# Two FFN down projections: eight of eleven double inner blocks as products of a seven-product block scheme

## The chip, the cores and the metric

The kernel runs on one core of one Trainium2 chip. The time is the device time of one launch in microseconds (us); the median of several runs is compared. Engines are named as in the profile: PE (TensorE), PEld (its weight loads), DVE (VectorE), ACT (ScalarE), POOL (GpSimd), SP (SyncE, which issues most DMAs).

## The reference

One encoder layer over two requests with the same weights, 256 and 512 tokens, D = 1024, D_FF = 2816, all in float32:

```python
x = layer_norm(a * x + 0.5 * swiglu(x, ffn1_w_gu, ffn1_w_down))
x = layer_norm(a * x + parallel_mixer(x, ...))
x = layer_norm(a * x + memory_cross_attention(x, mem, ...))
x = layer_norm(a * x + 0.5 * swiglu(x, ffn2_w_gu, ffn2_w_down))

def swiglu(x, w_gu, w_down):
    gate, up = jnp.split(x @ w_gu, 2, axis=-1)
    return (jax.nn.silu(gate) * up) @ w_down
```

The parts that matter here are the two down projections: h (768 x 2816) times w_down (2816 x 1024).

## The kernel before

All 768 tokens (512 of stream S and 256 of stream P) are worked on together. A float32 product is made of three matmuls in the format fp32r: each operand is split into a high part (cast by ACT, L87, tiles wh, hq, Vh) and a low part (operand minus high part, L88, by DVE or POOL, tiles wl, hq), and high x high, high x low and low x high are added in PSUM.

An FFN (`ffn_fast`, n = 1 or 2) has 22 inner blocks j of 128 hidden columns. For each j, a gate/up block (`block`, `products`) computes gate and up by a seven-product scheme: seven products of 12 matmuls 128x384, in the order P1, P5, P6, P3, P7, P2, P4. ACT copies partial sums out of PSUM (tiles snap), DVE adds (sum), ACT takes silu (sil), DVE multiplies (h), and `gated` splits h into hq (high by ACT, low by POOL) and sends it to DRAM (hspill, 768 KB), all but the last four j, which stay in SBUF (`keep`). Weights of the next block come in two loads of 512 KB (raw); `weights_of` makes sums of their halves on DVE (tiles tt, L330 to L338) and splits seven operands of 128x512, five low parts on DVE and two (P3, P2) on POOL. The first blocks (j = 0 to 2) of the first FFN are plain blocks beside the preparation of the token sums (tiles S1 to S4, L1096 to L1102); that part is called its front.

The down projection follows directly. A double inner block kp is two j's. Its weights are two halves of 512 output columns, each a load of 512 KB (raw, `load_w`) split by ACT (wh) and POOL (wl). `down_group` takes groups of blocks ([9, 10, 0], [1, 2, 3], [4, 5]): for each half it adds all blocks of the group in six PSUM banks (one per tile of 128 tokens; dn), 36 matmuls 128x512 per block and half, then DVE adds the banks to acc (L211, L213). Blocks other than 9 and 10 first read their hidden tiles back (hr, 768 KB). `down_last` does the last three blocks [6, 7, 8] tile by tile, with the layer norm of a finished tile beside the matmuls of the next. acc's old values (the residual) come in six loads issued by ACT.

The order on each engine is set by the tile framework that builds the program: it places instructions by dependencies and its own estimate of when they can start. SP works its queue in that order, and an instruction that waits holds up those behind it. Pools are given back tile by tile (`reuse_waits="tile"`), so a load into a new pool can wait for the last reader of the tile that had the memory before.

The mixer, between, starts with the same kind of seven-product blocks (tiles mS1 to mS4, acc as scratch) and `values()`, which makes V from weights split by ACT and POOL and is copied out of PSUM by DVE.

Of the kernel before, what the change touches and what calls it, by code (L numbers as in the profile page):

```python
# [7 lines left out]
F32 = mybir.dt.float32  # L8
# [50 lines left out]
def _encoder(ctx, tc, nc, io, out, dbg):  # L59
# [161 lines left out]
    def down_group(wdn, kps, hh, hl, first, after_loads=None):  # L221

        for half in range(2):
            pss = {(s.name, t): psum(nid("dn")) for s in STREAMS for t in range(s.nt)}
            for kp in kps:
                w = load_w(wdn[kp, half])
                for s in STREAMS:
                    for t in range(s.nt):
                        down(pss[s.name, t][:], s, t, w, kp, hh, hl, kp == kps[0], kp == kps[-1])
            if half == 0 and after_loads:  # L230
                after_loads()
            for s in STREAMS:
                for t in range(s.nt):
                    add_acc(s, t, half, pss[s.name, t][:], first)

    def down_last(wdn, kps, hh, hl, fp, i):

# [52 lines left out]
    def seven(X, pool, more, tt, snap_t, sum_t):  # L290

        unit = [None, None, 2]
        turn = [0]

        def raw():
            turn[0] += 1
            if (turn[0] - 1) % (3 + more) < 3:
                return wp.tile([128, 1024], F32, tag="raw", bufs=3, name=nid("raw"))
            return pool.tile([128, 1024], F32, tag="raw", bufs=more, name=nid("raw"))


# [12 lines left out]
        lo, hi = slice(0, 512), slice(512, 1024)  # L314

        def weights(wg, wu):

            rg, ru = raw(), raw()
            for r, w in ((rg, wg), (ru, wu)):
                if len(w.shape) == 4:  # L320
                    r4 = r[:].rearrange("p (a b c) -> p a b c", a=4, b=2)
                    for z in range(2):
                        nc.sync.dma_start(r4[:, :, z, :], w[:, :, z, :])
                else:
                    nc.sync.dma_start(r[:], w)
            V, G = nc.vector, nc.gpsimd
            t = [tt() for _ in range(4)]
            b = {}
            b["P1"] = operand(rg[:, lo], V)
            V.tensor_tensor(t[0], rg[:, lo], ru[:, lo], op=ALU.add)  # L330
            b["P5"] = operand(t[0], V)
            V.tensor_tensor(t[1], t[0], ru[:, hi], op=ALU.add)
            b["P6"] = operand(t[1], V)
            b["P3"] = operand(ru[:, hi], G)
            V.tensor_tensor(t[2], ru[:, lo], ru[:, hi], op=ALU.add)  # L335
            b["P7"] = operand(t[2], V)
            b["P2"] = operand(rg[:, hi], G)
            V.tensor_tensor(t[3], t[1], rg[:, hi], op=ALU.add)  # L338
            b["P4"] = operand(t[3], V)
            return b  # L340

        LEFT = {"P1": "A11", "P2": "A12", "P3": "S4", "P4": "A22", "P5": "S1", "P6": "S2", "P7": "S3"}

        def product(p, b, ps, start):
            tiles(X[LEFT[p]], b[p], ps, start)

        def tiles(a, w, ps, start, ks=range(4)):
            (ah, al), (wh, wl) = a, w
            for k in ks:
                c = slice(k * 128, (k + 1) * 128)  # L350
                st, sp_ = start and k == 0, k == 3
                for n, (l, r) in enumerate(((wh, ah), (wh, al), (wl, ah))):
                    nc.tensor.matmul(ps, l[:, c], r[:, k, :], start=st and n == 0, stop=sp_ and n == 2,  # L353
                                     skip_group_check=True)

        def snap(ps, nm):
            t = snap_t()
            ins = nc.scalar.activation(t, ps, AF.Copy)
            if nm == "p1":
                marks["act"] = ins.ins  # L360
            return t

        def added(ps, t, nm):
            o = sum_t()
            ins = nc.vector.tensor_tensor(o, t, ps, op=ALU.add)  # L365
# [24 lines left out]
        return operand, weights, tiles, products, (lo, hi)  # L390

    def ffn_fast(n, i, front, order6, src, groups, last):

        wgu, wdn = io[f"ffn{n}_gu"], io[f"ffn{n}_dn"]
        dr = dp.tile([128, NFB, 2, TT], F32, name=f"hspill{n}")
        right = ExitStack()
        hp = right.enter_context(tc.tile_pool(name=f"hkeep{n}", bufs=1, reuse_waits="tile", side="right"))
        left = ExitStack()
# [28 lines left out]
            marks["dve"] = ins.ins  # L427
            gated(j, h32)

        def gated(j, h32, eng=nc.gpsimd):  # L430
            q = hp.tile([128, 2, TT], F32R, tag="hq", bufs=4, name=nid("hq"))
            split(q[:, 0, :], q[:, 1, :], h32[:], eng)
            keep[j] = q
            if j < NFB - 4:
                nc.sync.dma_start(dr[:, j, :, :], q[:].bitcast(F32))

        def plain_weights(j):
            rg, ru = [wp.tile([128, 1024], F32, tag="raw", bufs=3, name=nid("raw")) for _ in range(2)]
# [23 lines left out]
            gated(j, h32)  # L462

        nx, ws = front(locals())
        for j in range(nx, NFB):
            block(j, ws)
            if j + 1 < NFB:
# [12 lines left out]
        def place(j, q):  # L480
            for s in STREAMS:
                for t in range(s.nt):
                    c = order6.index(s.t0 + t) * 128
                    hh[s.name, t, j], hl[s.name, t, j] = q[:, 0, c:c + 128], q[:, 1, c:c + 128]

        with tc.tile_pool(name=f"down{n}", bufs=1, reuse_waits="tile") as f2:
            for j in range(NFB - 4, NFB):
                place(j, keep[j])

            def load_h(js):  # L490
                for j in js:
                    q = f2.tile([128, 2, TT], F32R, tag="hr", bufs=6, name=nid("hr"))
                    nc.sync.dma_start(q[:].bitcast(F32), dr[:, j, :, :])
                    place(j, q)

            def load_acc():
                for t in range(6):
                    late_load(acc_[:, t, :], src[:, t, :])

            for gi, kps in enumerate(groups):  # L500
                load_h([j for kp in kps for j in (2 * kp, 2 * kp + 1) if j < NFB - 4])
                down_group(wdn, kps, hh, hl, gi == 0, None if gi else load_acc)
            load_h([j for kp in last for j in (2 * kp, 2 * kp + 1)])
            down_last(wdn, last, hh, hl, f2, i)
        right.close()


    def mixer(i):
# [53 lines left out]
        for b in (0, 2, 1, 3):  # L562
            small(b, H2, ws[b])

        def values(ts):
# [12 lines left out]

        slots = [o_[:, t, :] for t in range(6)] + [v_[:, t, :] for t in range(3, 6)]
# [37 lines left out]
        values(range(3))  # L617
# [496 lines left out]
    def front2(env):  # L1114
# [22 lines left out]
        quarters(X)  # L1137
        w2 = load_w(wgu[2]) + load_w(wgu[NFB + 2])
        for k in range(4):
            x0 = hp.tile([128, 2, TT], F32, tag="hq", bufs=4, name=nid("x0"))  # L1140
# [5 lines left out]
            sums(X, (env["snap_t"], env["sum_t"]), k, *a)  # L1146
        w3 = env["weights"](3)
        for j in range(2):
            env["gated"](j, h01[j], nc.vector)
        env["plain_block"](2, w2)  # L1150
        return 3, w3

    ffn_fast(1, 0, front1, [0, 2, 4, 1, 3, 5], io["x_tok"], ([9, 10, 0], [1, 2, 3], [4, 5]), [6, 7, 8])
    mixer(1)
    x3 = dp.tile([128, 6, D], F32, name="x3")
    with tc.tile_pool(name="lnx", bufs=1) as lp, tc.tile_pool(name="xa", bufs=1, reuse_waits="tile") as ap:
# [128 lines left out]
```

## Time and profile before

| | |
|---|---|
| median of 3 runs | 1823.75 us (1823.02 to 1828.21) |
| the profiled run | 1826.76 us, its span 1824.9 us, granted clock 0.994 |
| PE / PEld busy | 1796.2 us (98%) / 1647.8 us (90%) |
| DVE / ACT / POOL busy | 1154.2 (63%) / 716.1 (39%) / 640.6 us (35%) |
| DMA moved | 236.85 MB, mean 130 GB/s |
| POOL L88 wl<-raw,wh, all forms | 228 operations, 478.8 us |
| PE dn matmuls, the group of L106, L107, L108 | 438 each, 169 us each |

The profiled run is compared with its own span plus 1.9 us around it. Busy shares are averages over stages: PE is near 100% in nearly all of 40 slices, and what a slice waits for is read from the chain of waits and from the timeline. Times in a row of the timeline are the start in us from the span's start and the length in us; in brackets stands the idle time before and what ended it. Lengths of matmuls overlap, so their pitch is taken from start to start.

### The profile page before, as it was taken

How to read it: one execution, taken by the hardware profiler on the slowest of the kernel's cores; microseconds unless marked ns; L12 is line 12 of the kernel's file. 1: busy time of each engine (PE TensorE's matmuls, PEld its weight loads, DVE VectorE, ACT ScalarE, POOL GpSimd, SP SyncE). 2: the span in 40 equal slices, each digit the busy share in tenths (PEclk: the TensorE clock that was granted, in tenths of full speed). 3: DMA queues.
4: the chain of work that ended last, by engine and by line, in shares of the span. 5: the costliest groups of instructions: out<-in, count | busy, mean ns of one | idle time of the engine just before them, and what ended most of it. 6: DMA issues, size and time to landing. Idle time of an engine off the chain costs nothing.

```text
span 1824.9 us, 25380 instructions
## 1 busy us (share of the span) xinstructions
PE 1796.2 (98%) x9902; PEld 1647.8 (90%) x9902; DVE 1154.2 (63%) x1743; ACT 716.1 (39%) x1235; POOL 640.6 (35%) x362
## 2 busy tenths in 40 slices
PE   9999999999999999999999999999999999999998
PEld 8999999888889999888888888889899999998886
DVE  8788888212479554578654943485697788861136
ACT  6445444211135444555222254335354444441111
POOL 3333333432225112522244253243553333342212
PEclk9999999999999999999999999999999999999999
DMA  5333332635332333311363252246333333336441
GB/s 190 134 122 122 131 130 86 254 127 173 129 117 65 127 133 123 125 36 47 116 231 116 68 198 70 81 172 186 121 116 134 122 122 122 122 105 251 162 140 69
DMA packets 69335, 236.85 MB, mean 130 GB/s; under 512 B 7744, under 2 KB 13120, under 8 KB 69216
## 3 DMA queue, kind: packets, MB, share of 16 engines
q1 hardware_dynamic: 64032, 220.04, 35.1%
q10 hardware_dynamic: 5184, 15.21, 2.2%
q8 instruction: 77, 1.26, 0.3%
q14 instruction: 42, 0.34, 0.1%
HBM read 189.60 MB, written 45.61 MB: 129 GB/s over the span
## 4 chain that ended last, share of the span: by engine, by line
PE 71%; DVE 9%; ACT 1%; issue 1%; DMA 0%; POOL 0%; DVEq 0%; ACTq 0%
PE px L353 13%; PE py L353 7%; PE dn L108 7%; PE dn L107 7%; PE dn L106 7%; PE pt L107 4%; PE pt L106 4%; PE pt L108 4%; PE pz L353 3%; PE to L108 2%; PE to L107 2%; PE to L106 2%; DVE acc L172 1%; PE pp L353 1%; PE V L106 1%; PE V L107 1%
## 5 line engine op out<-in xcount | busy, mean ns | idle before, releaser
L88 POOL TENSOR_TENSOR wl<-raw,wh 128x1024 fp32r<-128x1024 f32 (+1 forms) x228 | 478.8, 2102 | 805.3 <-ACT wh L87 748.8
L87 ACT ACTIVATE wh<-raw 128x512 fp32r<-128x512 f32 (+2 forms) x313 | 260.5, 833 | 509.0 <-PE dn L108 195.2
L88 POOL TENSOR_TENSOR hq<-h,hq 128x768 fp32r<-128x768 f32 x42 | 86.1, 2050 | 252.5 <-ACT hq L87 132.6
L106 PE MATMUL pt<-xh,wh 128*128 128x512 f32 (+2 forms) x512 | 173.4, 339 | 0.0
L107 PE MATMUL pt<-xl,wh 128*128 128x512 f32 (+2 forms) x512 | 172.6, 337 | 0.0
L108 PE MATMUL pt<-xh,wl 128*128 128x512 f32 (+2 forms) x512 | 172.2, 336 | 0.0
L106 PE MATMUL dn<-wh,hr 128*128 128x512 f32 (+1 forms) x438 | 169.4, 387 | 0.0
L107 PE MATMUL dn<-wl,hr 128*128 128x512 f32 (+1 forms) x438 | 169.2, 386 | 0.0
L108 PE MATMUL dn<-wh,hr 128*128 128x512 f32 (+1 forms) x438 | 169.1, 386 | 0.0
L88 DVE TENSOR_TENSOR wl<-raw,wh 128x512 fp32r<-128x512 f32 (+2 forms) x85 | 111.8, 1320 | 82.9 <-ACT wh L87 82.8
L88 DVE TENSOR_TENSOR wl<-tt,wh 128x512 fp32r<-128x512 f32 x156 | 132.0, 882 | 4.5 <-ACT wh L87 3.9
L213 DVE TENSOR_TENSOR acc<-acc,dn 128x512 f32<-128x512 f32 (+1 forms) x73 | 49.2, 678 | 126.8 <-PE dn L108 126.6
L87 ACT ACTIVATE wh<-tt 128x512 fp32r<-128x512 f32 x156 | 93.5, 624 | 71.9 <-POOL wl L88 48.2
L106 PEld LDWEIGHTS pt<-xh,wh 128*128 128x128 f32 x512 | 97.4, 190 | 9.8 <-issue 0.5
L108 PEld LDWEIGHTS pt<-xh,wl 128*128 128x128 f32 x512 | 97.2, 190 | 9.0
L107 PEld LDWEIGHTS pt<-xl,wh 128*128 128x128 f32 x512 | 97.3, 190 | 8.7 <-issue 0.2
L107 PEld LDWEIGHTS dn<-wl,hr 128*128 128x128 f32 x438 | 82.3, 188 | 16.7
L106 PEld LDWEIGHTS dn<-wh,hr 128*128 128x128 f32 x438 | 82.3, 188 | 16.7
L108 PEld LDWEIGHTS dn<-wh,hr 128*128 128x128 f32 x438 | 82.3, 188 | 16.5
L425 DVE SCALAR_TENSOR_TENSOR h<-sil,sum 128x384 f32<-128x384 f32 x78 | 53.1, 683 | 61.3 <-ACT sil L424 61.3
L335 DVE TENSOR_TENSOR tt<-raw 128x512 f32<-128x512 f32 x39 | 87.8, 2252 | 0.0
L353 PE MATMUL px<-xh,wh 128*128 128x384 f32 x232 | 78.3, 337 | 2.5 <-DVE sum L365 2.5
(360 smaller groups left out, 4747.7 us busy)
## 6 DMA issues: line engine op xcount, KB each, us to landing
raw<-in_ffn_gu_dram SPq DMA_DIRECT2D x84, 512.0 KB, 3.5
hspill<-hq SPq DMA_DIRECT2D x36, 768.0 KB, 3.2
hr<-hspill SPq DMA_DIRECT2D x36, 768.0 KB, 5.5
raw<-in_ffn_dn_dram SPq DMA_DIRECT2D x44, 512.0 KB, 3.5
raw<-in_w_mix_dram SPq DMA_DIRECT2D x32, 512.0 KB, 3.5
raw<-in_w_xk_dram SPq DMA_DIRECT2D x16, 512.0 KB, 3.5
raw<-in_w_xv_dram SPq DMA_DIRECT2D x16, 512.0 KB, 4.0
raw<-in_w_xq_dram SPq DMA_DIRECT2D x16, 512.0 KB, 3.6
```

The lines of the kernel that those rows point to most:

```text
L87: nc.scalar.activation(hi, src, AF.Copy)
L88: (lo_eng or nc.vector).tensor_tensor(lo, src, hi.bitcast(F32), op=ALU.subtract)
L106: nc.tensor.matmul(o, lh, rh, start=start, stop=False)
L107: nc.tensor.matmul(o, lh, rl, start=False, stop=False)
L108: nc.tensor.matmul(o, ll, rh, start=False, stop=stop)
L172: nc.vector.scalar_tensor_tensor(Ah, Ah, mv[:, 0:1], g[h][:], ALU.subtract, ALU.mult)
L213: nc.vector.tensor_tensor(A, A, ps, op=ALU.add)
L335: V.tensor_tensor(t[2], ru[:, lo], ru[:, hi], op=ALU.add)
L353: nc.tensor.matmul(ps, l[:, c], r[:, k, :], start=st and n == 0, stop=sp_ and n == 2, skip_group_check=True)
L425: ins = nc.vector.scalar_tensor_tensor(h32[:, half * HT:(half + 1) * HT], sil[:], -0.5, u, ALU.mult, ALU.mult)
```

## The change

Three things change.

1. **`down_seven`** takes the place of `down_group`. Blocks 9, 10 and 1 to 6 are done as four pairs of the list groups ((9,10), (1,2), (3,4), (5,6); the loop writes one pair per index d). Each kp's two j's, two token halves of 384 (three tiles; order6 lists them) and two column halves form 2x2 blocks, and seven products take the place of eight: 18 matmuls 128x512 per product and pair. `direct` operands are hidden tiles (kept for d = 0, else read back, ao, 768 KB), `summed` operands are sums of hidden blocks (read back as sr, 384 KB, and split by ACT and DVE into ao). A weight quadrant is one load of 512 KB (128x2x512, in pieces of 2 KB); sums of quadrants are made on DVE in T (or in the loaded tile), and all low parts are made on DVE. Three sets of PSUM banks (x, z, y) take the products; `add` puts them into acc. `down_last` does [0, 7, 8]; its hidden tiles are loaded by `ahead()` before the last product.
2. **`gated`** makes the sums after every odd j of a paired block: four DVE operations 128x384 (hs) and four spills of 192 KB (sspill). hq's low part is made on DVE. The spills of the last pair are collected in `late` and are written, in the code, behind the first two products.
3. **POOL's seven-product work goes to DVE**: the low parts of P3 and P2 in gate/up blocks and mixer blocks, and of the first `values()`; `values()` is copied out of PSUM by ACT. acc comes in four lots of three loads of 256 KB.

Of the diff, with what is unchanged left out:

```diff
+    def down_seven(n, wdn, pairs, keep, dr, sd, order6, load_acc, late, ahead):
...
+            raw = [pool.tile([128, 1024], F32, name=nid("raw7")) for _ in range(2)]
+            T = {d: pool.tile([128, 1024], F32, name=nid("T")) for d in range(nd)}
+            bank = [psum(nid("dn")) for _ in range(8)]
+            x, z, y = bank[0:3], bank[3:6], bank[6:8] + bank[3:4]
...
+            def loaded(q, d):
+                turn[0] += 1
+                if turn[0] % 5 < 2:
+                    r = raw[turn[0] % 5]
+                else:
+                    r = wp.tile([128, 1024], F32, tag="raw", bufs=3, name=nid("raw"))
...
+            def direct(t, par, d):
+                if d == 0:
+                    return [keep[2 * kp + par][:, t] for kp in pairs[d]]
+                a = ring()      # ao, 4 buffers
+                nc.sync.dma_start(a[:].bitcast(F32), dr[:, t, par, kp:kp + 2])
...
+            def summed(s, d):
+                r = pool.tile([128, 2, HT], F32, tag="sr", bufs=3, name=nid("sr"))
+                nc.sync.dma_start(r[:], sd[:, s, kp:kp + 2])
+                a = ring()
+                split(a[:, :, 0, :], a[:, :, 1, :], r[:])
...
+            for d in own[:-1]:
+                P1(d)
+                if d == 0:
+                    load_acc(0, 0)
+                P2(d)
+            P2(own[-1])
+            P1(own[-1])
+            for spill in late:
+                spill()
+            for d in early:
+                quadrant(T[d][:], B11, d)
+            load_acc(1, 1)
+            add(0, 0, z)
+            add(0, 0, x)
+            for d in sums_:
+                V.tensor_tensor(T[d][:], T[d][:], loaded(B12, d), op=ALU.add)
+                product(y, summed(0, d), weight(T[d][:]), d == sums_[0], d == sums_[-1])
+            load_acc(0, 1)
+            add(1, 1, y)
+            for d in sums_:
+                b22 = loaded(B22, d)
+                V.tensor_tensor(T[d][:], T[d][:], b22, op=ALU.add)
+                product(x, summed(1, d), weight(T[d][:]), False, d == sums_[-1])
+                if d == sums_[-1]:
+                    add(0, 1, x)
+                product(y, summed(2, d), weight(b22), False, d == sums_[-1])
+            load_acc(1, 0)
+            add(0, 1, y)
+            for d in sums_:
+                b12, b22 = loaded(B12, d), loaded(B22, d)
+                V.tensor_tensor(b12, b12, b22, op=ALU.add)
+                product(x, summed(3, d), weight(b12), False, d == sums_[-1])
+            add(1, 1, x)
+            ahead()
+            for d in own:
+                V.tensor_tensor(T[d][:], T[d][:], loaded(B21, d), op=ALU.add)
+                product(x, direct(1, 1, d), weight(T[d][:]), False, d == own[-1])
+            add(1, 0, x)
...
-            b["P3"] = operand(ru[:, hi], G)
+            b["P3"] = operand(ru[:, hi], V)
-            b["P2"] = operand(rg[:, hi], G)
+            b["P2"] = operand(rg[:, hi], V)
...
+            if par and kp not in last:
+                s_ = [glob["hs"].tile([128, HT], F32, tag="hs", bufs=3, name=nid("hs")) for _ in range(4)]
+                V.tensor_tensor(s_[3][:], a11, a21, op=ALU.subtract)
+                V.tensor_tensor(s_[0][:], a22, a21, op=ALU.subtract)
+                V.scalar_tensor_tensor(s_[1][:], s_[0][:], -1.0, a11, ALU.mult, ALU.subtract)
+                V.scalar_tensor_tensor(s_[2][:], s_[1][:], -1.0, a12, ALU.mult, ALU.subtract)
+                def spill():
+                    for x in (3, 0, 1, 2):
+                        nc.sync.dma_start(sd[:, x, kp, :], s_[x][:])
+                if j == NFB - 1:
+                    late.append(spill)
+                else:
+                    spill()
...
-                w = load_w(io["w_v"][kp])
+                w = load_w(io["w_v"][kp], lo_eng)
-                nc.vector.tensor_copy(v_[:, t, :], ps[:])
+                nc.scalar.activation(v_[:, t, :], ps[:], AF.Copy)
-    ffn_fast(1, 0, front1, ..., ([9, 10, 0], [1, 2, 3], [4, 5]), [6, 7, 8])
+    ffn_fast(1, 0, front1, ..., ((9, 10), (1, 2), (3, 4), (5, 6)), [0, 7, 8])
```

What this makes of the queues shows in the built programs. A name's last number counts tiles; hq, hs and raw are as above.

SP's queue before, from the last loads of gate/up weights of the first FFN into the down projection:

```order
L435 DMA hspill_83<-hq_2775 128x1536
L325 DMA raw_3207<-in_ffn_gu_dram 128x1024
L325 DMA raw_3206<-in_ffn_gu_dram 128x1024
L96 DMA raw_3371<-in_ffn_dn_dram 128x1024
L96 DMA raw_3413<-in_ffn_dn_dram 128x1024
L96 DMA raw_3455<-in_ffn_dn_dram 128x1024
L96 DMA raw_3515<-in_ffn_dn_dram 128x1024
```

SP's queue after, at the same place:

```order
L582 DMA sspill_84<-hs_3140 128x384
L582 DMA sspill_84<-hs_3141 128x384
L238 DMA raw_3550<-in_ffn_dn_dram 128x2x512
L582 DMA sspill_84<-hs_3438 128x384
L582 DMA sspill_84<-hs_3435 128x384
L582 DMA sspill_84<-hs_3436 128x384
L582 DMA sspill_84<-hs_3437 128x384
L238 DMA raw_3459<-in_ffn_dn_dram 128x2x512
L265 DMA ao_3524<-hspill_83 128x1536
```

Before, weights of the down projection follow the last gate/up weights. After, the weights of the second to fourth steps (raw_3498, raw_3522, raw_3550) stand earlier, and the weight of the first step, raw_3459, stands behind the four spills of the last pair. In the second FFN two loads of hr, in two pieces each, stand among these spills as well, the second of them directly ahead of the first step's weight.

DVE before, from the end of the last gate/up block of the first FFN:

```order
L365 TENSOR_TENSOR sum_3323<-snap_3251,pz_3310 128x384
L425 SCALAR_TENSOR_TENSOR h_3337<-sil_3338,sum_3294 128x384
L425 SCALAR_TENSOR_TENSOR h_3337<-sil_3341,sum_3308 128x384
L211 SCALAR_TENSOR_TENSOR acc<-acc,dn_3365 128x512
L211 SCALAR_TENSOR_TENSOR acc<-acc,dn_3366 128x512
```

DVE after, at the same place:

```order
L484 TENSOR_TENSOR sum_3411<-snap_3339,pz_3398 128x384
L545 SCALAR_TENSOR_TENSOR h_3425<-sil_3426,sum_3382 128x384
L545 SCALAR_TENSOR_TENSOR h_3425<-sil_3429,sum_3396 128x384
L576 TENSOR_TENSOR hs_3435<-h_3425,h_3284 128x384
L577 SCALAR_TENSOR_TENSOR hs_3436<-hs_3435,h_3284 128x384
L88 TENSOR_TENSOR hq_3432<-h_3425,hq_3432 128x2x384
L578 SCALAR_TENSOR_TENSOR hs_3437<-hs_3436,h_3425 128x384
L88 TENSOR_TENSOR wl_3474<-raw_3459,wh_3473 128x1024
L88 TENSOR_TENSOR wl_3501<-raw_3498,wh_3500 128x1024
```

The three sums of the last pair and hq's low part now stand between the last h and the low part of the first step's weight (wl_3474), and that ahead of those of the next steps.

DVE before, at the front of the first FFN:

```order
L1100 SCALAR_TENSOR_TENSOR sum_365<-snap_364,x_115 128x384
L1102 TENSOR_TENSOR sum_366<-x_115 128x384
L330 TENSOR_TENSOR tt_495<-raw_491,raw_492 128x512
L88 TENSOR_TENSOR S3l_104<-sum_366,S3h_103 128x384
L332 TENSOR_TENSOR tt_496<-tt_495,raw_492 128x512
L88 TENSOR_TENSOR wl_500<-tt_495,wh_499 128x512
```

DVE after, at the same place:

```order
L1263 SCALAR_TENSOR_TENSOR sum_366<-snap_365,x_116 128x384
L88 TENSOR_TENSOR hq_294<-h_287,hq_294 128x2x384
L1265 TENSOR_TENSOR sum_367<-x_116 128x384
L449 TENSOR_TENSOR tt_496<-raw_492,raw_493 128x512
L88 TENSOR_TENSOR wl_509<-raw_493,wh_508 128x512
L88 TENSOR_TENSOR S3l_105<-sum_367,S3h_104 128x384
L88 TENSOR_TENSOR wl_501<-tt_496,wh_500 128x512
```

hq's low part and the low part of a plain weight half (wl_509), which POOL had, stand in DVE's row.

More of the change, by code (lines that the diff above doesn't have):

```diff
@@ L219, in down, with quadrant, weight, ring @@
             tok_mm(ps, w, kk, hh[s.name, t, j], hl[s.name, t, j], first and kk == 0, stop and kk == 1, cols)
[L221 to L234, printed above, removed]
+    def down_seven(n, wdn, pairs, keep, dr, sd, order6, load_acc, late, ahead):
+        with tc.tile_pool(name=f"seven{n}", bufs=1, reuse_waits="tile") as pool:
+            V = nc.vector
+            nd = len(pairs)
+            raw = [pool.tile([128, 1024], F32, name=nid("raw7")) for _ in range(2)]
+            turn = [0]
+            T = {d: pool.tile([128, 1024], F32, name=nid("T")) for d in range(nd)}
+            bank = [psum(nid("dn")) for _ in range(8)]
+            x, z, y = bank[0:3], bank[3:6], bank[6:8] + bank[3:4]
+            def quadrant(dst, q, d):
+                row, half = q
+                kp = pairs[d][0]
+                nc.sync.dma_start(dst.rearrange("p (a c) -> p a c", a=2),
+                                  wdn[kp:kp + 2, half, :, row * 512:row * 512 + 512].rearrange("a p c -> p a c"))
+            def loaded(q, d):
[4 more added lines that the diff above has]
+                    r = wp.tile([128, 1024], F32, tag="raw", bufs=3, name=nid("raw"))
+                quadrant(r[:], q, d)
+                return r[:]
+            def weight(src):
+                h = wp.tile([128, 1024], F32R, tag="wh", bufs=5, name=nid("wh"))
+                l = wp.tile([128, 1024], F32R, tag="wl", bufs=5, name=nid("wl"))
+                split(h[:], l[:], src)
+                return h, l
+            def ring():
+                return pool.tile([128, 2, 2, HT], F32R, tag="ao", bufs=4, name=nid("ao"))
+            def direct(t, par, d):
+                if d == 0:
+                    return [keep[2 * kp + par][:, t] for kp in pairs[d]]
+                a = ring()
+                kp = pairs[d][0]
+                nc.sync.dma_start(a[:].bitcast(F32), dr[:, t, par, kp:kp + 2])
+                return [a[:, k] for k in range(2)]
+            def summed(s, d):
+                r = pool.tile([128, 2, HT], F32, tag="sr", bufs=3, name=nid("sr"))
+                kp = pairs[d][0]
+                nc.sync.dma_start(r[:], sd[:, s, kp:kp + 2])
+                a = ring()
+                split(a[:, :, 0, :], a[:, :, 1, :], r[:])
+                return [a[:, k] for k in range(2)]
+            def product(ps, a, w, start, stop):
+                wh, wl = w
+                for t in range(3):
+                    c = slice(t * 128, t * 128 + 128)
+                    for k in range(2):
+                        o = slice(k * 512, k * 512 + 512)
+                        ah, al = a[k][:, 0, c], a[k][:, 1, c]
+                        for m, (l, r) in enumerate(((ah, wh), (ah, wl), (al, wh))):
+                            nc.tensor.matmul(ps[t][:], l, r[:, o], start=start and k == 0 and m == 0,
+                                             stop=stop and k == 1 and m == 2, skip_group_check=True)
+            seen = set()
+            def add(c, half, ps):
+                op = ALU.subtract if c == half == 1 or c < half else ALU.add
+                for t in range(3):
+                    A = acc_[:, order6[3 * c + t], half * 512:half * 512 + 512]
+                    if (c, half) in seen:
+                        V.tensor_tensor(A, A, ps[t][:], op=op)
+                    else:
+                        V.scalar_tensor_tensor(A, A, ALPHA, ps[t][:], ALU.mult, op)
+                seen.add((c, half))
+            acc_ = glob["acc"]
+            B11, B21, B12, B22 = (0, 0), (1, 0), (0, 1), (1, 1)
+            own = list(range(nd))
+            sums_ = own[1:] + own[:1]
+            early = own[:2]
+            def P1(d):
+                if d in early:
+                    src = loaded(B11, d)
+                else:
+                    quadrant(T[d][:], B11, d)
+                    src = T[d][:]
+                product(x, direct(0, 0, d), weight(src), d == own[0], d == own[-1])
+            def P2(d):
+                product(z, direct(0, 1, d), weight(loaded(B21, d)), d == own[0], d == own[-1])
+            for d in own[:-1]:
[8 more added lines that the diff above has]
+            for d in early:
+                quadrant(T[d][:], B11, d)
+            load_acc(1, 1)
[25 more added lines that the diff above has]
+            add(1, 0, x)
@@ L464, in ffn_fast @@
         nx, ws = front(locals())
+        glob["hs"] = left.enter_context(tc.tile_pool(name=f"hsum{n}", bufs=1, reuse_waits="tile"))
         for j in range(nx, NFB):
@@ L482, in place, with load_acc, load_h @@
                 for t in range(s.nt):
-                    c = order6.index(s.t0 + t) * 128
-                    hh[s.name, t, j], hl[s.name, t, j] = q[:, 0, c:c + 128], q[:, 1, c:c + 128]
-        with tc.tile_pool(name=f"down{n}", bufs=1, reuse_waits="tile") as f2:
[L487 to L503, printed above, removed]
+                    c = order6.index(s.t0 + t)
+                    x = slice(c % 3 * 128, c % 3 * 128 + 128)
+                    hh[s.name, t, j], hl[s.name, t, j] = q[:, c // 3, 0, x], q[:, c // 3, 1, x]
+        def load_acc(c, half):
+            for t in order6[3 * c:3 * c + 3]:
+                x = slice(half * 512, half * 512 + 512)
+                late_load(acc_[:, t, x], src[:, t, x])
+        js = [j for kp in last for j in (2 * kp, 2 * kp + 1)]
+        hlp = ExitStack()
+        def load_h(js, pool, tag, bufs):
+            for j in js:
+                q = pool.tile([128, 2, 2, HT], F32R, tag=tag, bufs=bufs, name=nid("hr"))
+                for t in range(2):
+                    nc.sync.dma_start(q[:, t].bitcast(F32), dr[:, t, j % 2, j // 2])
+                place(j, q)
+        if n == 1:
+            ahead = lambda: load_h(js[:4], hp, "hq", 4)
+        else:
+            lp = hlp.enter_context(tc.tile_pool(name="hlast", bufs=1, reuse_waits="tile"))
+            ahead = lambda: load_h(js, lp, "hr", 6)
+        down_seven(n, wdn, groups, keep, dr, sd, order6, load_acc, late, ahead)
+        with tc.tile_pool(name=f"down{n}", bufs=1, reuse_waits="tile") as f2:
+            if n == 1:
+                load_h(js[4:], f2, "hr", 2)
             down_last(wdn, last, hh, hl, f2, i)
+        hlp.close()
         right.close()
```

40 lines of the change are left out of this document (28 added, 12 removed).

## The prediction

> **What bounds the kernel now.** I read the page first, then TensorE's waits, then the timeline around the places that the change opens.
>
> ```profile
> PE 1796.2 (98%) x9902; PEld 1647.8 (90%) x9902; DVE 1154.2 (63%) x1743; ACT 716.1 (39%) x1235; POOL 640.6 (35%) x362
> ```
>
> ```profile
> PE px L353 <- ACT snap L358: 6.1, 3, 4.5
> PE K L108 <- DVE wl L88: 3.9, 2, 2.1
> PE px L353 <- DVE sum L365: 2.5, 1, 2.5
> ```
>
> TensorE works in 98% of the span and hardly ever waits (columns: us in total, times, longest). So a removed matmul is worth its pitch, and a new wait of TensorE costs its full length. A matmul's duration overlaps the next one's; the pitch is the distance of the starts:
>
> ```profile
> 360.20 0.39 PE L106 MATMUL dn<-wh,hr 128*128 128x512 f32 x1
> 360.42 0.39 PE L107 MATMUL dn<-wl,hr 128*128 128x512 f32 x1
> 360.65 0.39 PE L108 MATMUL dn<-wh,hr 128*128 128x512 f32 x1
> ```
>
> Two pitches are 0.45 us; a 128x512 matmul costs 0.227 us (0.225 to 0.23).
>
> **Fewer matmuls.** One double inner block takes 2 halves x 2 inner parts x 6 token tiles x 3 = 72 matmuls, a pair 144. Seven products of 3 tiles x 2 x 3 = 18 make 126. Eight pairs in the kernel save 8 x 18 = 144 matmuls: -32.7 us. Matmuls that read kept hidden tiles run a little slower (0.23, starts 339.22 and 339.45 below); their number hardly changes between the versions, so I take nothing, with +7 as the end if all 1008 new ones ran so.
>
> **A new wait at the start of each down projection.** Before, the projection follows the last gate/up block without a gap, because its first weights are asked for 7.6 us earlier:
>
> ```profile
> 331.63 11.55 SPq L96 DMA_DIRECT2D raw<-in_ffn_dn_dram  x4
> ```
>
> ```profile
> 339.04 0.34 PE L353 MATMUL px<-A22h,wl 128*128 128x384 f32 x1
> 339.22 0.39 PE L106 MATMUL dn<-wh,hq 128*128 128x512 f32 x1
> 339.45 0.39 PE L107 MATMUL dn<-wl,hq 128*128 128x512 f32 x1
> ```
>
> In the change the weight of the first product, raw_3459, stands on SP behind the four spills of the last pair's sums, and those wait for DVE work that follows the end of the last block. ACT and DVE have this weight ahead of those of the next products, and TensorE runs in order, so nothing else can start. How long after a block's end (call it E) its last h is done shows at an ordinary block, which ends at 221.84:
>
> ```profile
> 221.67 0.33 PE L353 MATMUL px<-A22h,wl 128*128 128x384 f32 x1
> 221.84 0.33 PE L353 MATMUL px<-A11h,wh 128*128 128x384 f32 x1
> ```
>
> ```profile
> 222.10 0.49 ACT L424 ACTIVATE sil<-px 128x384 f32<-128x384 f32 x1 [0.97 <-PE px L353]
> ```
>
> ```profile
> 222.63 0.56 DVE L425 SCALAR_TENSOR_TENSOR h<-sil,sum 128x384 f32<-128x384 f32 x1 [0.90 <-ACT sil L424]
> 223.10 0.68 DVE L330 TENSOR_TENSOR tt<-raw,raw 128x512 f32<-128x512 f32 x1
> 223.82 0.69 DVE L332 TENSOR_TENSOR tt<-tt,raw 128x512 f32<-128x512 f32 x1
> ```
>
> The steps behind it are priced by these groups (after the bar: busy us and mean ns; the next two by tile: min/median/max ns; the last: KB and us from issue to landing):
>
> ```profile
> L365 DVE TENSOR_TENSOR sum<-snap,pz 128x384 f32<-128x384 f32 x39 | 21.6, 554 | 42.1 <-PE pz L353 42.1
> L88 DVE TENSOR_TENSOR wl<-raw,wh 128x1024 fp32r<-128x1024 f32 x26 | 34.2, 1318 | 59.9 <-ACT wh L87 59.8
> L87 ACT ACTIVATE wh<-raw 128x1024 fp32r<-128x1024 f32 x154 | 163.2, 1060 | 472.6 <-PE dn L108 195.2 <-PE to L108 81.1 <-issue 49.7
> L213 DVE TENSOR_TENSOR acc<-acc,dn 128x512 f32<-128x512 f32 x71 | 48.3, 686 | 124.8 <-PE dn L108 124.7
> ```
>
> ```profile
> L435 SPq DMA_DIRECT2D hspill<-hq x36: 319/327/425, 38.2 to 1580.6; - x36
> L88 DVE TENSOR_TENSOR hq<-h,hq x2: 943/944/944, 1354.5 to 1355.4; 128x768 fp32r<-128x768 f32 x2
> ```
>
> ```profile
> hr<-hspill SPq DMA_DIRECT2D x36, 768.0 KB, 5.5
> raw<-in_ffn_dn_dram SPq DMA_DIRECT2D x44, 512.0 KB, 3.5
> ```
>
> DVE is free for the next operation at E+1.26. Two sums of 0.55 end at E+2.4, hq's low part (0.94) at E+3.3, the last sum at E+3.9. SP issues its spill (0.33) and raw_3459 at E+4.2, which lands 3.5 later at E+7.7. ACT's cast (1.06) brings E+8.8, DVE's low part (1.3) E+10.1. The third matmul needs it and would have started at E+0.47: 9.6 us, some 10.0 with handovers. Behind such a gap the granted clock is halved. Columns as above; first and last of the slow run, and the two behind it, at two gaps of before:
>
> ```profile
> 48.71 0.69 PE L353 MATMUL px<-S2h,wh 128*128 128x384 f32 x1 [4.49 <-ACT snap L358]
> 49.19 0.52 PE L353 MATMUL px<-S2l,wh 128*128 128x384 f32 x1
> ...
> 53.99 0.39 PE L353 MATMUL py<-S4l,wh 128*128 128x384 f32 x1
> 54.22 0.34 PE L353 MATMUL py<-S4h,wl 128*128 128x384 f32 x1
> ```
>
> ```profile
> 597.06 0.69 PE L353 MATMUL px<-xh,wh 128*128 128x384 f32 x1 [2.52 <-DVE sum L365]
> 597.55 0.52 PE L353 MATMUL px<-xl,wh 128*128 128x384 f32 x1
> ...
> 600.11 0.40 PE L353 MATMUL px<-xh,wh 128*128 128x384 f32 x1
> 600.34 0.34 PE L353 MATMUL px<-xl,wh 128*128 128x384 f32 x1
> ```
>
> 16 matmuls at about 0.32 where 0.17 is normal lost 2.4 us; at the second gap 9 lost 1.4. I take 2.1 behind the longer gap: 12.1 us in the first FFN. In the second, two pieces of hr (384 KB each) also stand between the spills and the weight: +0.7 (two issues) to +2 (5.5 against 3.5 above), I take 1.4: 13.5. Together **+25.6**, with ends 17 (each landing 2 us quicker and almost no slow clock) and 31 (landing as hr's, 5.5).
>
> The Trainium skill, "TensorE: Matmul & The Clock Gate", Part 1 on the clock gate, has the clock return after one window of about 3.4 us of work; by that each gap would lose 1.7 us instead of 2.1, and the sum would be 0.8 lower. The rows differ from it on both sides (5.3 and 3.1 us).
>
> **Inside the seven products.** A projection has 28 steps of 18 matmuls, 4.09 us each, 114 us. Beside them DVE has 28 low parts of weights and 16 sums of weights at about 1.3, 16 low parts of summed activations at 0.94 and 21 additions to acc at 0.69: 87 us. DMA moves 30 weights of 0.52 MB, 9 ao of 0.79, 16 sr of 0.39, 12 acc pieces of 0.26 and 6 hr of 0.79: 37 MB. What the queues deliver shows in the start of the first projection before (last column GB/s), where TensorE worked all the time:
>
> ```profile
> 340.00:350.00 10.00, 10.00 (x45) 8.02 (x44) 2.48 (x1) 2.64 (x4) 5.21 (x3) 1.00 0.88 320
> 350.00:360.00 10.00, 10.00 (x45) 8.11 (x44) 1.38 (x2) 1.06 (x1) 3.83 (x2) 1.00 1.01 417
> 360.00:370.00 10.00, 10.00 (x45) 8.16 (x44) 2.75 (x4) 1.06 (x1) 2.41 (x1) 1.00 0.97 375
> ```
>
> At their mean, 371, 37 MB take 100 us of the 114: hidden. The tightest loop is the fourth (sums of both right quadrants): DVE 4 x (1.3 + 0.94 + 1.3) + 6 additions = 18.3 us against 16.4, with buffers filled ahead by the looser loop before. I take **+3** for both projections (ends 0 and +15).
>
> **GpSimd freed.** Where GpSimd and DVE work together, DVE's operations stretch, at both fronts where TensorE waits for DVE:
>
> ```profile
> 36.36 2.20 DVE L1100 SCALAR_TENSOR_TENSOR sum<-snap,x 128x384 f32<-128x384 f32 x1
> ...
> 591.41 4.07 DVE L88 TENSOR_TENSOR wl<-acc,wh 128x512 fp32r<-128x512 f32 x3
> ```
>
> Operations of the first size take 0.55 above, three of the second about 2.1 (0.68 each). At the first FFN's front the change drops the GpSimd work but gives DVE hq's low part and two or three weights' (about 2): of the 4.5 us wait I take 1.5 off, with its slow clock kept (ends +1 and -6.9, all gone). At the mixer's front the wait of 2.5 us and the 1.4 of slow clock go: -4 (ends 0 and -4.5). Together **-5.5**.
>
> **Gate/up blocks.** Two of them, an even and an odd one:
>
> ```profile
> 221.84:250.96 29.12, 29.12 (x169) 29.12 (x169) 23.69 (x28) 13.98 (x26) 10.60 (x6) 1.00 0.37 127
> ```
>
> DVE has 28 operations: undisturbed 18 x 0.72 + 10 x 0.47 = 17.7 us (pitches from 223.10 to 223.82 and 222.63 to 223.10), so 6 are stretch by GpSimd. The change takes the stretch away and adds four low parts of weights (2.9), two of hq (1.9) and four sums (1.9): 24.4 of 29.1. TensorE stays the bound: +0.6 for now and then a late sum in the odd block (ends 0 and +11).
>
> **Sum:** -32.7 + 25.6 + 3 - 5.5 + 0.6 = -9.0 us. The profiled run took 1826.8 us (1824.9 span and 1.9 around it), 3 above the median; I put the difference on the median, 1823.75: **1815 us**.
>
> **Rivals.**
> - *The start waits are shorter.* For it: both landing and clock could be at their low ends, 17 us, and both fronts' waits could go fully. -32.7 + 17 + 3 - 9 = -22: 1802. Against it: the chain of DVE, SP, DMA, ACT, DVE is serial and each link is a row. If the wait does not arise at all, about 1786.
> - *DMA holds the products* (slower than before). 37 MB in 114 us need 323 GB/s; the 320 of the row 340 to 350 is just under it, and a load waits until its buffer is free. At 290 GB/s 37 MB take 128 us, +14 per projection in place of the +3 for both: -9 - 3 + 28 = +16, 1840. It cancels the gain at 308 GB/s (120 us, +6 per projection). Against it: the mean of 371.
> - *DVE holds the odd gate/up blocks*, 0.7 us in each of 16: +11, and the sum is about +2: 1825, no change. Against it: 24.4 of 29.1.
>
> **Chances.** Forecast 0.5 (own range 1807 to 1823), shorter start waits 0.2, DMA 0.15, odd blocks 0.12, others 0.03. A difference below 0.3% (5.5 us) is about what cannot be told from none. Faster by more: 0.2 and 0.7 of the forecast's 0.5, with little else: 0.56. Within: the rest of the forecast and most of the odd blocks, 0.25. Slower: 0.19. The range reaches from 1797, inside the shorter waits, to 1836, inside the DMA rival.
>
> **What would show it.** Matmul count down by 144. TensorE's waits lead with dn on ACT's wh and DVE's wl, twice, 9 to 14 us from the last px to the third dn, half clock behind. SP's issue of that raw some 4 us after the last px. Then steps of 4.1 us without gaps, the front's 2.5 us wait of px on sum gone, DVE's 128x512 group at L335 near 680 ns. I am wrong if the first dn follows px at once (1790), or if dn waits for sr, ao or wl throughout the products.

## The result, and the profile after

The changed kernel takes 1811.0 us (median of 4 runs, 1809.75 to 1814.35), the kernel before 1825.0 us on the same chip: a ratio of 0.992 with a 95% interval of 0.9906 to 0.9935. So it is faster, by 0.8%. The prediction said 1815, and the time lies in its range. The profiled run took 1809.75 us (its span 1808.0 us), 17.0 less than the profiled run before, which took 1826.76. The page's line of engines, and the first rows of TensorE's waits:

```profile
PE 1762.3 (97%) x9758; PEld 1618.6 (90%) x9758; DVE 1216.4 (67%) x2035; ACT 763.8 (42%) x1297; POOL 321.7 (18%) x186
```

```profile
PE dn L284 <- ACT wh L87: 20.8, 2, 11.9
PE px L472 <- ACT snap L477: 4.3, 2, 3.5
PE K L108 <- DVE wl L88: 4.0, 2, 2.3
```

There are 144 matmuls fewer, GpSimd's work is halved, the mixer's wait of px on sum has gone from the list, and two new waits of dn lead it. The timeline around the first of them, where the last gate/up block of the first FFN ends at 336.08 (E, the start of its last matmul and one pitch of 0.17):

```profile
335.90 0.34 PE L472 MATMUL px<-A22h,wl 128*128 128x384 f32 x1
...
336.33 0.49 ACT L544 ACTIVATE sil<-px 128x384 f32<-128x384 f32 x1 [0.97 <-PE px L472]
...
336.86 0.56 DVE L545 SCALAR_TENSOR_TENSOR h<-sil,sum 128x384 f32<-128x384 f32 x1 [0.90 <-ACT sil L544]
...
338.04 2.25 SPq L582 DMA_DIRECT2D sspill<-hs  x3
...
339.39 0.55 DVE L578 SCALAR_TENSOR_TENSOR hs<-hs,h 128x384 f32<-128x384 f32 x1
...
340.39 0.38 SPq L238 DMA_DIRECT2D raw<-in_ffn_dn_dram  x1
...
344.00 1.06 ACT L87 ACTIVATE wh<-raw 128x1024 fp32r<-128x1024 f32 x1 [5.70 <-DMA raw<-in_ffn_dn_dram]
...
345.08 1.23 DVE L88 TENSOR_TENSOR wl<-raw,wh 128x1024 fp32r<-128x1024 f32 x1 [5.15 <-ACT wh L87]
...
345.11 1.22 PE L284 MATMUL dn<-wh,hq 128*128 128x512 f32 x2 [8.87 <-ACT wh L87]
...
346.37 0.79 PE L284 MATMUL dn<-wl,hq 128*128 128x512 f32 x1
```

This is the predicted chain, link by link: last sum done at E+3.9, raw issued at E+4.3, landed at E+7.9, low part ready and the third matmul started at E+10.3 (predicted 10.1). In the second FFN, E is 1621.23, and SP has loads of hr among the spills:

```profile
1625.48 0.94 SPq L653 DMA_DIRECT2D hr<-hspill  x2
1626.76 0.38 SPq L238 DMA_DIRECT2D raw<-in_ffn_dn_dram  x1
...
1632.20 1.06 ACT L87 ACTIVATE wh<-raw 128x1024 fp32r<-128x1024 f32 x1 [8.76 <-DMA raw<-in_ffn_dn_dram]
...
1634.57 0.80 PE L284 MATMUL dn<-wl,hq 128*128 128x512 f32 x1
```

Raw is issued at E+5.5, 1.2 later than in the first FFN, and lands after 5.4 us instead of 3.6: the third matmul starts at E+13.3, 3.0 later.

Once started, the products run without gaps. Busy time by engine in the stretch of the 504 matmuls of the first projection's products, from their first start, in the changed kernel (then granted clock, DMA share, GB/s):

```profile
345.11:462.72 117.61, 117.57 (x504) 96.43 (x505) 79.59 (x82) 44.66 (x47) 4.79 (x2) 0.97 0.84 305
```

504 matmuls at 0.227 are 114.4 us; the 117.6 hold 3.1 of the start (0.8 until the third matmul, 2.3 of slow clock) and next to nothing else. The same view of the two gate/up blocks that answer to those of before, and of DVE's groups (after the bar: total us, mean ns) one of before and two of after:

```profile
222.10:251.22 29.12, 29.12 (x170) 29.12 (x169) 21.99 (x37) 14.20 (x27) 0.00 (x0) 1.00 0.41 147
```

```profile
L335 DVE TENSOR_TENSOR tt<-raw 128x512 f32<-128x512 f32 x39 | 87.8, 2252 | 0.0
```

```profile
L88 DVE TENSOR_TENSOR wl<-tt,wh 128x512 fp32r<-128x512 f32 x156 | 105.5, 689 | 2.2 <-ACT wh L87 0.5
...
L454 DVE TENSOR_TENSOR tt<-raw 128x512 f32<-128x512 f32 x39 | 26.8, 688 | 0.0
```

In the gate/up blocks DVE is busy 22.0 of 29.1 us, 1.7 less than before, with more work: its operations are no longer stretched (L335, now L454, 2252 to 688 ns). That GpSimd's work beside them had stretched them shows in the kernels between, described below: the same group takes 2257 ns in the mean with only hq's low part left on GpSimd (e3), 938 with only P3 and P2 there (e2) and 683 with neither (e9).

Where the time went, by stage. Each stage runs from the first start of its first group of matmuls to that of the next stage's (the last one to the start of the last matmul, some 8 us before the span's end), and the wait at a projection's start from the end of the last px, counted as E above, to the first dn, both from the timelines (us). "Others" is what the change does not touch, from the first FFN's layer norm to the mixer and through the attention. The runs of the experiments below stand beside it.

| stage | before | after | e1 | e2 | e3 | e4 | e5 | e6 | e7 | e8 | e9 |
|---|---|---|---|---|---|---|---|---|---|---|---|
| FFN1 front and blocks | 333.5 | 330.3 | 329.6 | 331.4 | 333.2 | 331.5 | 334.7 | 330.6 | 333.3 | 329.9 | 332.6 |
| wait | 0 | 9.0 | 0 | 9.7 | 0 | 0 | 0 | 9.2 | 0 | 0 | 0 |
| down 1 | 184.2 | 171.4 | 173.2 | 171.5 | 184.2 | 170.0 | 184.2 | 171.4 | 184.3 | 171.9 | 184.2 |
| mixer | 184.0 | 178.9 | 178.9 | 178.3 | 178.9 | 178.9 | 178.3 | 178.9 | 184.0 | 178.9 | 178.9 |
| FFN2 front | 56.0 | 54.0 | 54.0 | 54.0 | 56.0 | 54.0 | 56.0 | 54.0 | 56.0 | 54.0 | 56.0 |
| FFN2 blocks | 275.9 | 276.8 | 276.8 | 277.8 | 275.8 | 276.8 | 275.9 | 276.8 | 276.2 | 276.8 | 275.9 |
| wait | 0 | 12.1 | 0 | 11.4 | 0 | 0 | 0 | 9.4 | 0 | 0 | 0 |
| down 2 and end | 180.8 | 166.2 | 170.3 | 165.5 | 180.8 | 167.0 | 181.1 | 167.1 | 180.8 | 174.4 | 181.1 |
| others | 596.4 | 595.0 | 600.2 | 600.1 | 594.7 | 596.3 | 597.6 | 595.7 | 599.7 | 597.8 | 597.5 |

### The profile page after: what moved, and what is told of

It is laid out like the page before. It is cut to its first block, busy times and chain, and to the rows that moved or that the text cites. A ratio compares the mean times of both kernels' runs of the same rounds, so it can differ in the third digit from the quotient of the medians.

```text
span 1808.0 us, 25217 instructions
## 1 busy us (share of the span) xinstructions
PE 1762.3 (97%) x9758; PEld 1618.6 (90%) x9758; DVE 1216.4 (67%) x2035; ACT 763.8 (42%) x1297; POOL 321.7 (18%) x186
## 5 line engine op out<-in xcount | busy, mean ns | idle before, releaser
L88 POOL TENSOR_TENSOR wl<-raw,wh 128x1024 fp32r<-128x1024 f32 (+1 forms) x94 | 231.6, 2468 | 1319.7 <-ACT wh L87 1271.4
L88 DVE TENSOR_TENSOR wl<-raw,wh 128x512 fp32r<-128x512 f32 (+2 forms) x215 | 182.8, 853 | 99.6 <-ACT wh L87 99.3
L284 PE MATMUL dn<-wh,ao 128*128 128x512 f32 x600 | 185.4, 389 | 0.0
L284 PEld LDWEIGHTS dn<-wh,ao 128*128 128x128 f32 x600 | 112.6, 188 | 23.5
L284 PE MATMUL dn<-wl,ao 128*128 128x512 f32 x300 | 116.7, 389 | 0.0
L472 PE MATMUL px<-xh,wl 128*128 128x384 f32 x232 | 77.5, 334 | 0.0
L472 PE MATMUL px<-xl,wh 128*128 128x384 f32 x232 | 77.5, 334 | 0.0
L284 PEld LDWEIGHTS dn<-wl,ao 128*128 128x128 f32 x300 | 56.3, 188 | 11.8
L106 PE MATMUL dn<-wh,hr 128*128 128x512 f32 (+1 forms) x150 | 57.7, 385 | 0.0
L107 PE MATMUL dn<-wl,hr 128*128 128x512 f32 (+1 forms) x150 | 57.5, 383 | 0.0
```

Of the source, the lines that this page charges most:

```text
L88: (lo_eng or nc.vector).tensor_tensor(lo, src, hi.bitcast(F32), op=ALU.subtract)
L106: nc.tensor.matmul(o, lh, rh, start=start, stop=False)
L107: nc.tensor.matmul(o, lh, rl, start=False, stop=False)
L284: nc.tensor.matmul(ps[t][:], l, r[:, o], start=start and k == 0 and m == 0, stop=stop and k == 1 and m == 2, skip_group_check=True)
```

## The experiments

**The start waits: is it one load's place on SP's queue?** In e1 the first step's weight goes into a buffer that is free early, so that it is asked for with the last gate/up weights, and the hr loads are put behind the second step's ao.

```diff
-            turn = [0]
+            turn = [1]
...
-            ahead()
+            with tc.issue_after(gate):      # gate: the ao load of P2, d = 1
+                ahead()
```

> The ring of load buffers starts one turn later, so the first step's weight goes into a buffer that is free during the last gate/up block, and SP asks for it ahead of the last pair's spills; the hr loads stand behind the second ao load. Theory (the two start waits, 9.0 and 12.1 us with 3.0 and 2.6 of slow clock behind them, come only from that weight standing behind the spills): no gap from px to dn; the next limit is the first ao load, issued 4.3 us after the block's end and needed 8.2 after it, so 1 to 2 us remain per projection. 1811 - 26.7 + 3 = 1787. Rival (the products run without gaps only because the wait lets loads and low parts run ahead): the gaps come back inside the first two loops, 10 us or more per projection, 1800 or above.

It took 1796.4 us, 0.983 of before (0.9812 to 0.9848). Both start waits are gone: the first dn follows the last px at once. What is left in TensorE's list:

```profile
PE dn L284 <- DMA ao<-hspill: 4.7, 2, 2.5
...
PE dn L284 <- DVE acc L294: 1.9, 1, 1.9
```

The 1787 was not reached. The second step's ao is now what stands behind the spills on SP: 2.5 and 2.2 us, each with a slow clock behind it that cost 1.7 us more, and a wait on acc adds 1.9, where 3 had been allowed for all that would be left. Besides, the stages that no edit touches took 5 us more than in the run of after (others, 600.2 against 595.0; on this the last section). So the cause of the wait is shown, and the next wait that it had covered.

e4 takes that wait away too: four fixed ao tiles in memory that is free early, the last pair's spills on ACT's queue, and acc's first loads behind the second step.

```diff
+            aos = [pool.tile([128, 2, 2, HT], F32R, name=nid("ao")) for _ in range(4)]
...
-                        nc.sync.dma_start(sd[:, x, kp, :], s_[x][:])
+                        q.dma_start(sd[:, x, kp, :], s_[x][:])   # q: nc.scalar for the last pair
```

> The changed kernel with the first step's weight asked for early (as in e1) and, besides, four fixed ao tiles that lie where long finished memory is, the last pair's spills issued by ACT's queue, and the first acc loads placed behind the second step. If the two waits of the second step for its ao (2.5 and 2.2 us in e1) and the half clock behind them come only from ao's place on SP behind the spills, dn shows no wait above 1 us, and both projections lose 4 to 5 us each against e1: 1787 us (1784 to 1790). Rival: ACT, which now issues spills that wait for DVE, is held up itself and brings wh late: a wait of dn on ACT's wh returns, 1794 us or more.

Two rows of its timeline, at the transition, and the only row of dn above 1 us:

```profile
337.02 0.34 PE L479 MATMUL px<-A22h,wl 128*128 128x384 f32 x1
337.19 0.39 PE L288 MATMUL dn<-wh,hq 128*128 128x512 f32 x1
```

```profile
PE dn L288 <- DVE acc L298: 1.4, 1, 1.4
```

The projections are 3.2 and 3.3 us shorter than in e1, where 4 to 5 were forecast. No wait of dn on ACT's wh comes near the old ones (the list has 0.4 us), and the rival is out. The time is 1792.1 us, 0.9828 of before (0.9803 to 0.9853), outside the forecast of 1784 to 1790; by the ratios e4 cannot be told from e1, since the stages that neither edit touches differ by as much. Both are faster than before and than the changed kernel.

**The hr loads among the spills of the second FFN.** e6 is the changed kernel with only the second edit of e1 (`ahead()` behind the ao load).

> After, with the hr loads of both projections behind the second ao load of the products; nothing else moved. Theory (the second FFN's start wait is 3 us longer than the first's because two hr pieces stand in SP's queue ahead of the first weight): its wait falls from 12.1 to about 9.0 us, the first FFN's stays 9.0: 1808. Rival (the longer wait comes from the memory that this weight's buffer waits for): 12.1 stays, 1811.

The wait of the second FFN falls from 12.1 to 9.4 us, next to the first FFN's 9.2. So the hr loads cost 2.7 us of TensorE's wait, by the rows above through their issue and through the traffic they put beside raw's; the whole time (1809.1 in one run) is too coarse to tell.

**Is DMA near holding the products?** e8 is e4 with a copy of 256 KB in DRAM behind 26 of the 30 weight loads of the products (those that go through `loaded`).

```diff
+                with tc.issue_after(marks["w"]):
+                    x = dp.tile([128, 512], F32, name=nid("xtra"))
+                    nc.sync.dma_start(x[:], wdn[pairs[d][0], half, :, row * 512:row * 512 + 512])
```

> e4 with a copy of 256 KB from DRAM to DRAM issued behind each weight load of the seven-product part, whose result nobody reads: per projection at least 6.8 MB more beside 37 MB, 385 GB/s over the 114 us of the products. If the queues deliver the 371 to 417 GB/s of the fuller rows, the products stay hidden or lose at most 6 us per projection: 1787 to 1800 us. By the DMA rival of the prediction (a limit near 310 GB/s) each projection's products last at least 140 us: 1840 us or more.

The products of both projections in e4 and then in e8, and, inside the second projection of e8, two windows of 10 us and a row from the first of them:

```profile
337.19:453.20 116.01, 115.62 (x506) 94.39 (x506) 79.14 (x84) 43.88 (x47) 4.79 (x2) 1.00 0.84 303
1613.20:1731.10 117.90, 115.82 (x506) 94.28 (x505) 79.30 (x84) 43.99 (x47) 4.79 (x2) 1.00 0.87 316
```

```profile
335.60:453.00 117.40, 115.61 (x506) 94.44 (x506) 78.61 (x83) 43.98 (x47) 4.39 (x2) 1.00 0.94 342
1615.00:1739.60 124.60, 118.15 (x506) 95.11 (x505) 77.73 (x83) 43.86 (x47) 4.89 (x2) 0.99 0.91 336
```

```profile
1635.00:1645.00 10.00, 7.61 (x27) 5.59 (x26) 3.58 (x3) 3.06 (x3) 0.00 (x0) 0.83 1.04 405
1705.00:1715.00 10.00, 10.00 (x46) 8.29 (x45) 3.17 (x4) 1.78 (x2) 0.00 (x0) 1.00 1.03 402
```

```profile
1638.75 2.01 ACT L259 ACTIVATE wh<-raw 128x1024 fp32r<-128x1024 f32 x2 [6.43 <-DMA raw<-in_ffn_dn_dram]
```

With some 5 MB more in each stretch (GB/s times us: 35.2 against 40.2 MB, and 37.3 against 41.9) the products lose 1.4 and 6.7 us, and the one run took 1799.8. A limit at 290 to 308 GB/s is out: the queues moved 336 to 342 in the mean and 402 to 405 in single windows. There is an edge, though: in the first window the queues are full, ACT waits 6.4 us for a weight that DMA brings, and TensorE is busy 7.6 of 10 us, part of it at a lower clock (0.83 in the mean). In the second window the queues are just as full and TensorE loses nothing. So, as an estimate from the two means, the products of the changed kernel, at 305, have room of some 10%. The second projection's loss is just above the 6 that was allowed.

**What does freeing GpSimd bring, and which part of it?** Five kernels share this. e2 is the changed kernel with P3's and P2's low parts given back to GpSimd. The others are the kernel before with one part of the change: e3 has P3, P2 and the first `values()` moved off GpSimd, e5 `values()` alone, e7 hq's low part alone, e9 all three. With `values()` goes its second edit, the copies out of PSUM on ACT instead of DVE.

```diff
-            b["P3"] = operand(ru[:, hi], G)          # P2 likewise: e3, e9
+            b["P3"] = operand(ru[:, hi], V)
...
-        values(range(3))                             # e3, e5, e9
+        values(range(3), nc.vector)
...
-        def gated(j, h32, eng=nc.gpsimd):            # e7, e9
+        def gated(j, h32, eng=nc.vector):
```

> After, with the low parts of P3 and P2 on GpSimd again in gate/up and mixer blocks; all else as after. Theory (11 us of the gain lie outside the down projections and come from DVE no longer being stretched by GpSimd): front of the first FFN and the mixer's seven-product part lose again, and with the added sums DVE is near its limit in the odd blocks: 1811 + 9 = 1820, and more if odd blocks wait. Rival (those 11 us come from the other moves, hq on DVE or the new order): 1811 to 1813.

> Before, with part 3 of the change alone: P3 and P2 low parts on DVE, the first values() low parts on DVE, values() copied out by ACT; hq's low part stays on GpSimd, the down projections are unchanged. Theory: most of the 11 us: 1825 - 8 = 1817, the mixer's part 5 shorter. Rival: 1823 to 1825, then the gain outside the down projections needs hq on DVE.

> The kernel before with one edit: the first values() has its low parts on DVE and its copies out of PSUM on ACT; GpSimd keeps P3, P2, hq and the plain weights. If the mixer's gain of 5.2 us is due to values() alone, the mixer's stage falls from 184 to 179 us, all other stages stay, and the time falls by 5 us, to 0.997 of before. Rival: the gain comes from P3 and P2 (GpSimd no longer beside DVE in the seven-product blocks): the stage stays at 183 to 184, no change of the time.

> The kernel before with one edit: hq's low part is made by DVE instead of GpSimd. If the 2 us at each FFN's front that e3 did not bring come from this, the front of the second FFN falls from 56.0 to 54.0 us and the first FFN's gate/up stage from 333.5 to about 331.5: -4 us in all, 0.998 of before. Rival: they come from the new order of the loads; then no stage moves and the time stays.

> The kernel before with all three GpSimd edits (P3 and P2, the first values(), hq's low part) and no seven-product down projection. If the fronts gain because GpSimd as a whole has less to do, the second FFN's front falls from 56.0 to 54.0 us, the first FFN's gate/up stage from 333.5 to 331.4 or less, the mixer's stage to 179: -9 us in all, 0.995 of before, and below e3. Rival: the fronts' gain comes with the new code of the down projection, which changes the tiles of hq and the order in which the fronts' instructions are placed: both fronts stay as before, and the kernel takes what e3 takes, -5 to -7 us, 0.9965.

| | time, us | ratio to before | interval |
|---|---|---|---|
| e2 | 1815.4 | 0.9932 | 0.9917 to 0.9947 |
| e3 | 1818.8 | 0.9953 | 0.9939 to 0.9966 |
| e5 | 1819.9 | 0.9972 | 0.9958 to 0.9985 |
| e7 | 1828.4 | 1.0007 | 0.9994 to 1.0020 |
| e9 | 1818.6 | 0.9955 | 0.9937 to 0.9973 |

The mixer's stage decides: 184.0 wherever `values()` is as before (before, e7), 178.3 to 178.9 wherever it is changed, with P3 and P2 on GpSimd (e2, e5) or not. So `values()` alone brings the 5.2 us at the mixer, and e3 and e5 came out near their forecasts (1817; 0.997). P3 and P2 add nothing to it there; whether they alone would have brought it too, no run tests. They bring 1.0 us in the second FFN's blocks of the changed kernel (277.8 to 276.8) and nothing in those of the kernel before (275.9 and 275.8). The 1820 of e2 was not reached, and neither were the 1811 to 1813 of its rival: it took 4 us more than the changed kernel by medians, intervals overlapping, and of the 5.6 us between the profiled runs 5 lie in the stages that the edit does not touch (others, 600.1 against 595.0).

How `values()` does it shows on DVE ahead of the sum for which TensorE waited 2.5 us. Two rows before, between which the stretched row at 591.41 of the prediction stands, then two of e5:

```profile
588.74 1.87 DVE L576 COPY acc<-tb 128x512 f32<-128x512 f32 x3
...
595.40 0.54 DVE L365 TENSOR_TENSOR sum<-acc,py 128x384 f32<-128x384 f32 x1
```

```profile
588.70 4.69 POOL L88 TENSOR_TENSOR wl<-raw,wh 128x512 fp32r<-128x512 f32 x3
...
590.31 0.56 DVE L365 TENSOR_TENSOR sum<-acc,py 128x384 f32<-128x384 f32 x1 [1.02 <-PE py L353]
```

Before, DVE is late without a pause. In e5 it waits 1.0 us for TensorE ahead of the same sum, although GpSimd still makes the low parts of P3 and P2 there: the three copies (1.87 us) are gone, and the other work was done earlier. The two edits of `values()`, low parts and copies, were not run apart, so what each brings stays open.

The theory of e7 fell: hq's low part on DVE moves no front. That of e9 fell too: with all three edits the second FFN's front is still 56.0. e2 has it at 54.0, and what e2 has beyond e9's edits is the new down projection with its tiles of hq (it lacks that of P3 and P2). The waits that go with it, first in the kernel before, then in e9:

```profile
PE lt L191 <- DVE acc L177: 1.1, 2, 0.6
```

```profile
PE px L353 <- ACT snap L358: 4.7, 3, 3.3
...
PE lt L191 <- DVE acc L177: 1.1, 2, 0.6
```

In the changed kernel the waits of lt are gone from the list, and by the starts of the same matmuls 1.9 of the 2.0 us arise at these two groups of lt. So the 2 us at the second front come with the new code, not with a freer GpSimd; which of its lines does it was not taken further. At the first FFN e9 lowers the longest wait from 4.5 to 3.3 us, but its stage (332.6) is less than 1 us below before's, and kernels with one code differ there by 2 (329.6 to 331.5): of the 3.1 us that the changed kernel gains, the share of GpSimd stays open.

## Why the prediction was right, and where it was not

The sign and the two large terms held: a gain of matmuls, given back for the larger part as two start waits. The gain was forecast too small, 9 us against 14.0 between the medians and 17.0 between the two profiled runs; what is missing lies in the small terms, nearly all on one side. By terms, against the 17.0 us:

| term | predicted | measured | from |
|---|---|---|---|
| 144 matmuls | -32.7 | -33.0 | down 1 and 2, with the slow start of 3.1 and 2.5 taken out: -15.9 and -17.1 |
| start waits | +25.6 | +26.7 | 9.0 + 3.1 and 12.1 + 2.5 |
| inside the products | +3 | 0 | in the -33.0 |
| first FFN's front and blocks | -1.5 | -3.1 | stage |
| mixer's front | -4 | -5.2 | stage |
| second FFN's front | 0 | -2.0 | stage |
| gate/up blocks, second FFN | +0.6 for both | +1.0 | stage |
| others | 0 | -1.4 | stages |

- *Start waits.* The chain was right in each link, and in the first FFN to 0.1 us (12.1 both ways). The step that was off is hr's: +1.4 taken, with an end of 2, and 3.0 measured. The 1.4 lay between the issue alone (0.7) and the longer landing alone (2), as if only one of them came; in the rows above both do, the issue 1.2 later and the landing 1.8.
- *The slow clock.* 2.1 per gap was taken, and from the third matmul on 2.3 and 1.7 were lost. By the Trainium skill, "TensorE: Matmul & The Clock Gate", Part 1, with its one window of about 3.4 us of work, an estimate is 1.7 each: the mean of 2.0 lies between, and nothing hangs on the difference.
- *Inside the products.* The step that failed is the margin for DVE's tightest loop, 18.3 us against 16.4: buffers filled ahead carried all of it. That loop ran in 16.3 us, and its four sums of weights had been made on DVE in the loop before. DMA was priced nearly right (323 GB/s needed, 305 measured), and by e8 the rival's limit does not lie at 290 to 308.
- *GpSimd freed.* At the mixer the place was right: the 2.5 us wait and its slow clock went, as forecast. The rest of the -5.2, beyond the end of -4.5, are smaller waits ahead of it with their slow clock (0.5 of px on acc in the list of before), which were not counted. The mechanism is shown only in part: copies moved to ACT may have done as much as GpSimd's absence. At the first FFN -3.1 is twice the -1.5. By the starts of the same matmuls 1.9 of it lie at the longest wait and its slow clock, and 0.8 at a wait of the last block that no step of the prediction had; the share of GpSimd is open. The second FFN's front was taken at nothing, and its -2.0 come with the new code (e9).
- *Odd gate/up blocks.* DVE's 24.4 of 29.1 us was 22.0 over an even and an odd block, and the rival is out. The +1.0 in the second FFN is no late sum in odd blocks, so that the size is near the +0.6 by luck: the first block behind the front has two new waits on ACT's snap, and the last block has lost the one that it had. First the rows of after, then that of before:

```profile
1347.49 0.44 PE L472 MATMUL px<-S2h,wh 128*128 128x384 f32 x1 [0.82 <-ACT snap L477]
1350.72 0.44 PE L472 MATMUL py<-S4h,wh 128*128 128x384 f32 x1 [0.88 <-ACT snap L477]
```

```profile
1625.18 0.44 PE L353 MATMUL px<-S2h,wh 128*128 128x384 f32 x1 [1.02 <-ACT snap L358]
```

- *The rival "shorter start waits".* That chain is serial as argued. Its 1786 "if the wait does not arise" is what e4 (1792) comes near, by an edit that makes it not arise.

## What to carry to other kernels

Before counting what a cheaper scheme saves, look at the first load that it needs and at what stands before it in its queue: here one 512 KB load behind four spills gave back 27 of 33 us, and a buffer that was free earlier brought 15 of them back (e1), 19 with the next wait taken out too (e4), without touching the scheme. When an edit takes one wait away, read off which load or operand is next in line behind the same obstacle (here ao, 2.5 us). And compare stages rather than whole times when several kernels differ by 2 to 5 us, since untouched stages move by as much.

## What the runs showed of the hardware

The same wait of TensorE is followed by a halved clock in one run and not in another. In the attention one matmul of K waits 1.76 us in the kernel before and 1.75 us in the changed one, in code that the change does not touch. Its row, and the 3.5 us behind it, before and then after:

```profile
1046.75 0.38 PE L108 MATMUL K<-mh,wl 128*128 128x256 f32 x1 [1.76 <-DVE wl L88]
```

```profile
1047.00:1050.50 3.50, 3.50 (x20) 3.50 (x20) 3.47 (x10) 0.26 (x1) 0.00 (x0) 0.55 0.77 272
```

```profile
1034.32 0.38 PE L108 MATMUL K<-mh,wl 128*128 128x256 f32 x1 [1.75 <-DVE wl L88]
```

```profile
1034.32:1037.77 3.45, 3.45 (x29) 3.45 (x30) 3.42 (x12) 0.00 (x0) 0.00 (x0) 1.00 0.67 237
```

Before, 20 matmuls run in 3.5 us at a granted clock of 0.55; after, 29 at 1.00. The stage from K to V takes 28.36 us in the one case and 26.85 in the other, and in all eleven profiled runs it lies within 0.05 us of one of the two. So the same short wait costs 1.5 us more or not, by something that is not in the code of the place; what it is, no run here shows. This one place gives 1.5 of the 5.5 us over which "others" spreads.
